# A mixture-of-experts backbone: the first expert in the order of the others, its slot weights in parts, and the last two experts added on chip

## The chip, the cores and the metric

The kernel runs on one core of a Trainium2 chip. The time is that of the device for one execution, in microseconds (us); less is better. The engines are TensorE (PE, matmuls), VectorE (DVE), ScalarE (ACT), GpSimd (POOL), and the queue engine SP, which issues most of the loads.

## What is computed

Two layers of a backbone over 256 context tokens and 512 latent tokens of width 1024. Each layer is a token mixer and a mixture of experts, each added to the residual. The mixture, cut to what matters here:

```python
g_top = argmax(h @ rg_w + rg_b)              # 1 of 4 groups, weight g_w
top_vals, top_idx = lax.top_k(e_in, 2)       # 2 of its 8 experts
top_w = softmax(top_vals) * g_w
...
def run_block(tok, e):                       # rows tok of h, expert e of 32
    xb = h_pad[tok]
    return (silu(xb @ w_gate[e]) * (xb @ w_up[e])) @ w_down[e]
...
y = segment_sum(y_buf * buf_w[:, None], buf_tok)
```

Each expert has a gate and an up matrix of 1024x512 and a down matrix of 512x1024 in f32, 6 MB together. Layer 0 has 768 tokens, layer 1 only needs the 512 latent ones. All 32 experts are computed in both.

## The kernel before

**Experts.** Every expert gets a table of 96 slots (`CAP`). `slots` makes, for all experts at once, which token stands in which slot (`si`); `values` makes what weight it has (`sv`, and `v4` for tokens that find no slot): DVE splits the weights into three f16 parts (`rwt`), PE places them by selection matrices (`ptab`, L1117), DVE adds the parts (`tw`, `sv`). `fetch` (POOL, an indirect DMA) reads an expert's rows from HBM into `xg`, `turn` transposes them on PE, `turned` copies them to `xh` (DVE) and `xl` (ACT). `gate_up` is the gate or the up product (`pgate`, `pup`); `act_gate`, `act_mult` and `act_split` make the activation, `at`; `down_mm` is the down product (`pdn`), `down_out` scales it by the slot weight on ACT, `scatter` gates it on POOL and adds it to the residual rows `xs` in HBM by an indirect DMA.

**Weights.** The weights come in halves of 1 MB into 7 buffers (`raw`, `NR`). The order of the loads is written out, and `pump` issues the next one on SP when a buffer is given back and no more than `depth` are under way. A half becomes two f16 matrices: `hi_` on ACT (L1337), then `lo_` on DVE (L1342), which frees the buffer. The second half of a down matrix is used in f32 by PE (`native`). In this document lo(up 1a) is the DVE conversion of the first half of expert 1's up matrix, gate(31) the gate product of expert 31.

**Order.** Nothing is scheduled by a tool: each engine executes its instructions in the order of the code. For expert e the loop computes act_mult(e), gate(e+1), the conversions for e+1 and e+2, pdn(e), the transposed rows of e+2, and up(e+1). Expert 0 stands ahead of the loop, in an order of its own: slot weights, transposes of expert 1, pdn(0), gate(1), up(1). The last two experts:

- Experts 0 to 30 are added to `xs` by scatters; then `load_latent` loads the latent rows from `xs` (SP) into `xl`.
- Expert 31 is added on chip (`last_down`, `add_last`): selections `pes` (`make_sel`, four on POOL at expert 28) are transposed on PE (`pst`, L1434), its product is placed by matmuls (`pcm`, L1458), and DVE adds them to the loaded rows (L1461).
- Between up(31) and pdn(31) stands `overflow_blocks`: each engine loads the number of overflow blocks and branches (L1357) over a loop for tokens that found no slot. There are none for this input.

Of the kernel before, what the change touches and what calls it, by code (L numbers as in the profile page):

```python
# [8 lines left out]
F32 = mybir.dt.float32  # L9
# [9 lines left out]
D = 1024  # L19
# [5 lines left out]
NE = 32  # L25
# [16 lines left out]
def kernel(ctx: ExitStack, tc: tile.TileContext, a: dict, out: bass.AP):  # L42
# [16 lines left out]
    def W(shape, dt, name="wt"):  # L59
        return pw.tile(shape, dt, name=name, tag="W")  # L60
# [970 lines left out]
    class Route:  # L1031
# [89 lines left out]
        def values(self):  # L1121

            nt, tmp, oh, v4 = self.nt, self.tmp, self.oh, self.v4
            g0, o1, o2, tv = tmp[:, :, 56:60], tmp[:, :, 120:152], tmp[:, :, 152:184], tmp[:, :, 184:216]
            gs, w1, w2, ex = (tmp[:, :, 220 + i] for i in range(4))

            def bc(x, n=32):
                return x.unsqueeze(2).to_broadcast([128, nt, n])

            V.tensor_tensor(g0, self.L[:, :, 32:36], bc(tmp[:, :, 40], 4), op=ALU.subtract)  # L1130
            V.tensor_tensor(ex, tmp[:, :, 49], tmp[:, :, 48], op=ALU.subtract)
            A.activation(g0, g0, AF.Exp)
            A.activation(ex, ex, AF.Exp)
            V.tensor_tensor(v4[:, :, :, 0], oh, bc(tokv[:, 0:nt]), op=ALU.mult)
            V.tensor_reduce(gs, g0, axis=AX.X, op=ALU.add)
            V.tensor_scalar(w1, ex, 1.0, None, op0=ALU.add)
            V.reciprocal(gs, gs)
            V.reciprocal(w1, w1)
            V.tensor_tensor(w1, w1, gs, op=ALU.mult)
            V.tensor_tensor(w2, w1, ex, op=ALU.mult)  # L1140
            rs = []
            for k, (o, w) in enumerate(((o1, w1), (o2, w2))):
                V.scalar_tensor_tensor(tv, o, VS, bc(w), op0=ALU.mult, op1=ALU.mult)
                rs.append(W([128, nt, 3, 32], F16, "rwt"))
                for q in range(3):
                    V.tensor_copy(rs[k][:, :, q], tv)
                    if q < 2:
                        V.tensor_tensor(tv, tv, rs[k][:, :, q], op=ALU.subtract)
            for q in range(3):
                V.tensor_tensor(v4[:, :, :, q + 1], rs[0][:, :, q], rs[1][:, :, q], op=ALU.add)  # L1150
            pt = self.table(rs, 96)
            t = W([128, 96], F32, "tw")[0:CAP]
            V.tensor_copy(t, pt)
            V.tensor_tensor(t[:, 0:32], t[:, 0:32], t[:, 32:64], op=ALU.add)
            V.tensor_tensor(t[:, 0:32], t[:, 0:32], t[:, 64:96], op=ALU.add)
            V.tensor_scalar(self.sv[0:CAP, 0], t[:, 0:32], IWS / VS, None, op0=ALU.mult)

        def overflow(self):

# [60 lines left out]
    def turn(xg):  # L1220

        out = []
        for r in range(2):
            pt = pp.tile([128, KC, CAP], F16, name="pgx", tag="P")
            for c in range(KC):
                o = r * D + c * 128
                T.transpose(pt[:, c, :], xg[0:CAP, o:o + 128], ident16[0:CAP, 0:CAP])
            out.append(pt)
        return out

    def turned(pts):
        xh = W([128, KC, CAP], F16, "xh")
        xl = W([128, KC, CAP], F16, "xl")
        V.tensor_copy(xh, pts[0])  # L1234
        A.copy(xl, pts[1])  # L1235
        return xh, xl
# [29 lines left out]
    def act_mult(pu, sg):  # L1266

        V.scalar_tensor_tensor(sg[:, 0:2], pu[:, 0:2], IWS, sg[:, 0:2], op0=ALU.mult, op1=ALU.mult)
        V.tensor_tensor(sg[:, 2:4], pu[:, 2:4], sg[:, 2:4], op=ALU.mult)

    def act_split(sg):
        at = W([128, 2, 2, CAP], F16, "at")
        A.copy(at[:, 0], sg[:, 0:2])  # L1273
        V.tensor_tensor(at[:, 1], sg[:, 0:2], at[:, 0], op=ALU.subtract)
        return at

    def down_mm(w, raw, at, sg, n):

        hi, lo = w
        sl = slice(n * 512, (n + 1) * 512)  # L1280
        pt = P([128, 512], "pdn")
        for f in range(2):
            mm3(pt[0:CAP, :], at[:, 0, f, :], at[:, 1, f, :], hi[:, f, sl], lo[:, f, sl], f == 0, False)
        for f in range(2, 4):
            T.matmul(pt[0:CAP, :], lhsT=sg[:, f, :], rhs=raw[:, f - 2, sl], start=False, stop=(f == 3))  # L1285
        return pt

    def down_out(pt, wcol, yt, n):
        A.activation(yt[0:CAP, n * 512:(n + 1) * 512], pt[0:CAP, :], AF.Copy, scale=wcol)  # L1289
# [55 lines left out]
    def moe(l, h2, rt, pe0, nt, post_load=None):  # L1345
# [3 lines left out]
        def overflow_blocks():  # L1349
# [7 lines left out]
            with tc.If(nov > 0):  # L1357
                with tc.For_i(0, nov) as _i:
# [17 lines left out]
                    V.tensor_tensor(pm, posm, eqb, op=ALU.mult)  # L1376
                    V.tensor_reduce(pb[:, :, 0], pm, axis=AX.X, op=ALU.add)
                    V.tensor_scalar(pb[:, :, 0], pb[:, :, 0], bc[:, 3:4], None, op0=ALU.subtract)
                    vb = W([128, nt, 4], F16, "vb2")
                    for q in range(4):  # L1380
                        V.tensor_tensor(pm, v4[:, :, :, q], eqb, op=ALU.mult)
                        V.tensor_reduce(vf, pm, axis=AX.X, op=ALU.add)
# [36 lines left out]
                            mm3(pt[0:CAP, :], at[:, 0, f, :], at[:, 1, f, :], hi[:, f, sl], lo[:, f, sl], f == 0, f == 3)  # L1419
                        down_out(pt, sv[0:CAP, 1:2], yg[:, 0, :], n)  # L1420
                    scatter(l, yg, si[0:CAP, :1], gs, V)
                load_latent(nc.gpsimd)

        xl = []

        def load_latent(eng=nc.sync):
            for i in range(4):
                eng.dma_start(out=xl[i // 2][:, i % 2, :], in_=xs[l][i * 128:(i + 1) * 128, :])
# [58 lines left out]
        def rows_of(e):  # L1487
            yg = yes[e % 2]
            return yg, gate_rows(yg, rt.sv[0:CAP, 1, e:e + 1], g2r, nv)
# [16 lines left out]
        gate_up(convs.pop((l, 0, 1)), xe, put)  # L1506
        lo_()
        hi_(1, 1, 0)
        act_mult(put, sg)
        at = act_split(sg)  # L1510
        lo_()
        rt.values()
        hi_(1, 1, 1)
        yg, gs = rows_of(0)
        w, raw = convs.pop((l, 0, 2)), natives.pop((l, 0))
        xt_ = turn(xg[:, 1])
        for n in range(2):
            pt = down_mm(w, raw, at, sg, n)
            if n == 0:
                xe = turned(xt_)  # L1520
            down_out(pt, weight(0), yg[:, 0, :], n)
        lo_()
        scatter(l, yg, slot(0), gs, Q)
        pgt = P([128, 4, CAP], "pgate")
        gate_up(convs.pop((l, 1, 0)), xe, pgt)
        hi_(2, 0, 0)
        sg = act_gate(pgt)
        lo_()
        hi_(2, 0, 1)
        xt_ = turn(xg[:, 0])  # L1530
        xn = turned(xt_)
        lo_()
        hi_(1, 2, 0)
        native(1)
        lo_()
        put = P([128, 4, CAP], "pup")
        gate_up(convs.pop((l, 1, 1)), xe, put)
        hi_(2, 1, 0)
        lo_()
        hi_(2, 1, 1)  # L1540
        for e in (3, 4):
            fetch(l, xg[:, e % 2], slot(e))
        xe = xn
        pes = None
        for e in range(1, NE):

            nx, nx2 = e + 1 < NE, e + 2 < NE
            act_mult(put, sg)
            at = act_split(sg)
            if lows:  # L1550
                lo_()
            sgd = sg
            w, raw = convs.pop((l, e, 2)), natives.pop((l, e))
            yg, gs = rows_of(e)
            if e == NE - 2:
                st["depth"] = NR - 2
            if e == NE - 4:
                pes = W([128, nt, CAP], F16, "pe")
                make_sel(pes, posm[:, :, NE - 1:NE], range(4))
            if not nx:  # L1560
                break
            pgt = P([128, 4, CAP], "pgate")
            gate_up(convs.pop((l, e + 1, 0)), xe, pgt)
            if nx2:
                for hf in range(2):
                    hi_(e + 2, 0, hf)
                    lo_()
            sg = act_gate(pgt)
            hi_(e + 1, 2, 0)
            native(e + 1)  # L1570
            lo_()
            pt = down_mm(w, raw, at, sgd, 0)
            down_out(pt, weight(e), yg[:, 0, :], 0)
            if nx2:
                hi_(e + 2, 1, 0)
            pt = down_mm(w, raw, at, sgd, 1)
            down_out(pt, weight(e), yg[:, 0, :], 1)
            scatter(l, yg, slot(e), gs, Q)
            if nx2:
                xn = turned(turn(xg[:, e % 2]))  # L1580
                lo_()
                hi_(e + 2, 1, 1)
                if e + 4 < NE:
                    fetch(l, xg[:, e % 2], slot(e + 4))
            else:
                xl += [G([128, 2, D], F32, "xl") for _ in range(2)]
                load_latent()
                selT = sel_transposed(pes)
                if post_load:
                    post_load()  # L1590
            put = P([128, 4, CAP], "pup")
            gate_up(convs.pop((l, e + 1, 1)), xe, put)
            xe = xn
            if e == 8:
                rt.overflow()
        overflow_blocks()
        if l == 0:
            st["depth"] = 4
            conv_w("win", 1, 4, 0)
# [1 line left out]
        yh = last_down(w, raw, at, sgd, yg, NE - 1, gs)  # L1601
        if l == 0:
            scatter_rows(l, yg, slot(NE - 1))
        add_last(selT, yh)
        return xl

    iot1 = pc.tile([128, CAP], F16, name="iot1")
# [190 lines left out]
```

## Time and profile before

| | |
|---|---|
| median of 3 runs | 1833.77 us (1828.28 to 1836.45) |
| the profiled execution | 1832.03 us |
| its span | 1830.3 us |
| busy: PE, PEld, DVE, ACT, POOL | 88%, 64%, 74%, 56%, 56% |
| mean DMA rate over the span | 296 GB/s |
| overall granted clock of TensorE | 0.944 |

The span is from the first to the last instruction. A window lists the engines in the order of the table, with their instructions in brackets; PEclk is the granted clock of TensorE as a share of 2.4 GHz (0.50 is 1.2 GHz). The busy shares are means over stages with different limits: the mixture of layer 0 lies at about 372 to 982 us, that of layer 1 at 1239 to 1820.

### The profile page before, as it was taken

What the parts mean: (1) busy time and instruction counts of PE and PEld (TensorE: products, weight loads), DVE (VectorE), ACT (ScalarE), POOL (GpSimd) and SP (SyncE); (2) the same over time, 40 slices, a digit from 0 to 9 for tenths busy, and PEclk for the clock granted to TensorE, in tenths of its full rate; (3) what the DMA queues carried; (4) which work ended last, traced back from release to release, by engine and by line L of the source; (5) the groups of instructions that cost most, each with busy time, mean ns of one, the idle gap of its engine ahead of it and who ended that gap; (6) DMA issues with size and microseconds to landing.
All of it is one profiled execution on the core that took longest, in us unless ns stands there. A gap on an engine that the chain in (4) does not pass through costs nothing. (4 is left out here: it accounts for less than half of the span.)

```text
span 1830.3 us, 43421 instructions
## 1 busy us (share of the span) xinstructions
PE 1610.0 (88%) x19059; PEld 1178.2 (64%) x19059; DVE 1346.8 (74%) x1453; ACT 1020.0 (56%) x1040; POOL 1030.3 (56%) x530
## 2 busy tenths in 40 slices
PE   6999999868888999888788999977987988899896
PEld 3577775556676777676664667546766676777663
DVE  5665566778768998777778777786876876777664
ACT  4433342446666676565654444345766676766763
POOL 1222224556998899988895233252555455665553
PEclk9999999988999999999998999988999999999998
DMA  9635455569998999999994354747999999999993
GB/s 386 240 135 187 162 209 200 172 206 365 362 369 318 372 394 387 369 351 358 364 353 174 113 198 167 299 154 234 409 386 371 361 384 365 370 387 369 371 359 122
DMA packets 127293, 542.33 MB, mean 296 GB/s; under 512 B 21594, under 2 KB 22666, under 8 KB 91000
## 3 DMA queue, kind: packets, MB, share of 16 engines
q1 hardware_dynamic: 105384, 507.87, 72.9%
q0 software_dynamic: 18000, 20.56, 4.7%
q10 hardware_dynamic: 3712, 11.04, 1.6%
q8 instruction: 153, 2.51, 0.5%
q14 instruction: 44, 0.36, 0.1%
HBM read 538.72 MB, written 45.69 MB: 319 GB/s over the span
## 5 line engine op out<-in xcount | busy, mean ns | idle before, releaser
L1342 DVE SCALAR_TENSOR_TENSOR wlo<-raw,whi 128x2048 f16<-128x2048 f32 x248 | 599.1, 2447 | 187.6 <-ACT whi L1337 187.3
L1337 ACT ACTIVATE whi<-raw 128x2048 f16<-128x2048 f32 x248 | 472.6, 1910 | 292.6 <-DMA raw<-in_exp_w_up_dram 245.0
L420 PEld LDWEIGHTS <-wlo 128*128 128x128 f16 x4512 | 457.3, 101 | 156.1 <-issue 124.8
L418 PEld LDWEIGHTS <-whi 128*128 128x128 f16 x4512 | 458.2, 102 | 45.5 <-issue 16.3
L419 PEld LDWEIGHTS <-whi 128*128 128x128 f16 x4512 | 457.6, 101 | 41.7 <-issue 12.6
L419 PE MATMUL pgate<-xl,whi 128*128 128x96 f16 x2048 | 305.1, 219 | 114.1 <-ACT xl L1235 113.7
L418 PE MATMUL pgate<-xh,whi 128*128 128x96 f16 x2048 | 309.0, 219 | 5.8 <-DVE xh L1234 5.7
L420 PE MATMUL pgate<-xh,wlo 128*128 128x96 f16 x2048 | 305.1, 219 | 0.0
L1305 POOL TENSOR_TENSOR ye<-ye,modrow 96x512 f32<-96x512 f32 x62 | 161.9, 2612 | 239.0 <-ACT ye L1289 239.0
L418 PE MATMUL pup<-xh,whi 128*128 128x96 f16 x2048 | 266.3, 206 | 0.0
L420 PE MATMUL pup<-xh,wlo 128*128 128x96 f16 x2048 | 266.1, 206 | 0.0
L419 PE MATMUL pup<-xl,whi 128*128 128x96 f16 x2048 | 266.0, 206 | 0.0
L1285 PE MATMUL pdn<-raw,sg 128*96 128x512 f32 x512 | 246.0, 604 | 0.0
L1309 POOL DMA_INDIRECT xs<-ye,si x63 | 183.3, 2910 | 22.5 <-POOL ye L1305 17.5
L1342 DVE SCALAR_TENSOR_TENSOR wd<-raw,wd 128x2048 f16<-128x2048 f32 x64 | 165.9, 2592 | 15.6 <-ACT wd L1337 15.4
L1305 POOL TENSOR_TENSOR ye<-ye 96x512 f32<-96x512 f32 x62 | 137.1, 2222 | 56.0 <-ACT ye L1289 54.0
L1296 POOL TENSOR_SCALAR ye<-modrow,sv 96x1024 f32<-96x1024 f32 x32 | 145.2, 4538 | 1.3
L1285 PEld LDWEIGHTS pdn<-raw,sg 128*96 128x96 f32 x512 | 85.6, 167 | 90.6 <-issue 71.9
L1337 ACT ACTIVATE wd<-raw 128x2048 f16<-128x2048 f32 x64 | 122.2, 1909 | 22.0 <-DMA raw<-in_exp_w_down_dram 22.0
L405 DVE SCALAR_TENSOR_TENSOR wlo<-raw,whi 128x2048 f16<-128x2048 f32 (+1 forms) x36 | 85.3, 2373 | 40.3 <-ACT whi L404 40.3
L418 PE MATMUL pdn<-wd,at 128*96 128x512 f16 x256 | 100.1, 391 | 16.4 <-ACT at L1273 8.6
L1215 POOL DMA_INDIRECT xg<-hs,si x62 | 91.6, 1477 | 32.5 <-issue 20.3
(310 smaller groups left out, 3103.3 us busy)
## 6 DMA issues: line engine op xcount, KB each, us to landing
raw<-in_exp_w_gate_dram SPq DMA_DIRECT2D x128, 1024.0 KB
raw<-in_exp_w_up_dram SPq DMA_DIRECT2D x128, 1024.0 KB
raw<-in_exp_w_down_dram SPq DMA_DIRECT2D x128, 1024.0 KB
raw<-in_ada_w_dram SPq DMA_DIRECT2D x32, 1024.0 KB
raw<-in_w_in_dram SPq DMA_DIRECT2D x20, 1024.0 KB
raw<-in_ada_dram SPq DMA_DIRECT2D x16, 1024.0 KB
raw<-in_w_out_dram SPq DMA_DIRECT2D x8, 1024.0 KB
xs<-xr ACTq DMA_DIRECT2D x10, 512.0 KB
```

The lines of the kernel that those rows point to most:

```text
L405: V.scalar_tensor_tensor(lo, t, WS, hi, op0=ALU.mult, op1=ALU.subtract)
L418: T.matmul(o, lhsT=lh, rhs=rh, start=first, stop=False)
L419: T.matmul(o, lhsT=lh, rhs=rl, start=False, stop=False)
L420: T.matmul(o, lhsT=ll, rhs=rh, start=False, stop=last)
L1215: Q.indirect_dma_start(out=xg, out_offset=None, in_=hs[l], in_offset=bass.IndirectOffsetOnAxis(ap=si, axis=0), bounds_check=(6 - 2 * l) * ...
L1285: T.matmul(pt[0:CAP, :], lhsT=sg[:, f, :], rhs=raw[:, f - 2, sl], start=False, stop=(f == 3))
L1296: Q.tensor_scalar(gn, g2r[0:CAP, 1, :], ctx, None, op0=ALU.mult)
L1305: eng.tensor_tensor(yn, yn, gs[n], op=ALU.mult)
L1309: Q.indirect_dma_start(out=xs[l], out_offset=bass.IndirectOffsetOnAxis(ap=si, axis=0), in_=yg[0:si.shape[0], 0, :], in_offset=None, bounds ...
L1337: A.activation(hi[:, sl, :], t, AF.Copy, scale=WS)
L1342: V.scalar_tensor_tensor(lo, t, WS, hi, op0=ALU.mult, op1=ALU.subtract)
```

## The change

1. Expert 0 goes through the same loop as the others. Ahead of it the rows of expert 1 are transposed first, and `values` becomes a generator with three parts: the weights and their split; `ptab`, `tw`, `sv`; and `v4`. The first runs at the loop's entry, the second and third behind the first and second conversion after gate(1).
2. `overflow_blocks` stands at the start of expert 29's turn. The scratch for its values is a part of another tile.
3. Experts 30 and 31 are both added on chip. The latent rows are loaded ahead of gate(31), behind the scatter of expert 29. The selections of both (8) are made by DVE there, and transposed there by PE. Expert 30 is scattered as well, after `last_down`. Its `add_last` stands between up(31) and pdn(31), where the branch stood.
4. `depth` falls to `NR - 2` two experts earlier.

```diff
@@ values
+            yield
             pt = self.table(rs, 96)
...
             V.tensor_scalar(self.sv[0:CAP, 0], t[:, 0:32], IWS / VS, None, op0=ALU.mult)
+            yield
+            V.tensor_tensor(v4[:, :, :, 0], oh, bc(tokv[:, 0:nt]), op=ALU.mult)
+            for q in range(3):
+                V.tensor_tensor(v4[:, :, :, q + 1], rs[0][:, :, q], rs[1][:, :, q], op=ALU.add)
+            yield
@@ overflow_blocks
                     scatter(l, yg, si[0:CAP, :1], gs, V)
-                load_latent(nc.gpsimd)
@@ moe
         hi_(1, 1, 0)
-        act_mult(put, sg)
-        at = act_split(sg)
+        xe = turned(turn(xg[:, 1]))
         lo_()
-        rt.values()
         hi_(1, 1, 1)
...
-        for e in range(1, NE):
+        vals = rt.values()
+        for e in range(NE):
...
-            if e == NE - 2:
+            if e == NE - 4:
                 st["depth"] = NR - 2
-            if e == NE - 4:
-                pes = W([128, nt, CAP], F16, "pe")
-                make_sel(pes, posm[:, :, NE - 1:NE], range(4))
+            if e == NE - 3:
+                overflow_blocks()
             if not nx:
                 break
+            if e == 0:
+                next(vals)
+            if e == NE - 2:
+                xl += [G([128, 2, D], F32, "xl") for _ in range(2)]
+                load_latent()
+                sels = []
+                for k in (NE - 2, NE - 1):
+                    pe = W([128, nt, CAP], F16, "pe")
+                    make_sel(pe, posm[:, :, k:k + 1], range(4), V)
+                    sels.append(sel_transposed(pe))
+                if post_load:
+                    post_load()
             pgt = P([128, 4, CAP], "pgate")
             gate_up(convs.pop((l, e + 1, 0)), xe, pgt)
             if nx2:
                 for hf in range(2):
                     hi_(e + 2, 0, hf)
                     lo_()
+                    if e == 0:
+                        next(vals)
...
             else:
-                xl += [G([128, 2, D], F32, "xl") for _ in range(2)]
-                load_latent()
-                selT = sel_transposed(pes)
-                if post_load:
-                    post_load()
+                yh = last_down(w, raw, at, sgd, yg, e, gs)
+                scatter_rows(l, yg, slot(e))
...
-        overflow_blocks()
+        add_last(sels[0], yh)
...
-        add_last(selT, yh)
+        add_last(sels[1], yh)
```

**What it moves at the head.** The order on DVE in layer 0, before: two conversions (`wlo`, L1342: lo(gate 1b), lo(up 1a)) stand about the activation of expert 0 (`sg`, `at`); then the slot weights in one piece, to `tw` and `sv`, and the copy of expert 1's rows, `xh`.

```order
L1342 SCALAR_TENSOR_TENSOR wlo<-raw,whi 128x2048
L1268 SCALAR_TENSOR_TENSOR sg<-pup,sg 128x192
L1269 TENSOR_TENSOR sg<-pup,sg 128x192
L1274 TENSOR_TENSOR at<-sg,at 128x192
L1342 SCALAR_TENSOR_TENSOR wlo<-raw,whi 128x2048
L1130 TENSOR_TENSOR rtmp<-rtmp 128x6x4
...
L1150 TENSOR_TENSOR rv_2717<-rwt 128x192 x3
L1153 COPY tw<-ptab 96x96
...
L1234 COPY xh<-pgx 128x768
L1342 SCALAR_TENSOR_TENSOR wlo<-raw,whi 128x2048 x2
```

The same place on DVE after the change:

```order
L1345 SCALAR_TENSOR_TENSOR wlo<-raw,whi 128x2048
L1237 COPY xh<-pgx 128x768
L1345 SCALAR_TENSOR_TENSOR wlo<-raw,whi 128x2048
L1271 SCALAR_TENSOR_TENSOR sg<-pup,sg 128x192
...
L1345 SCALAR_TENSOR_TENSOR wlo<-raw,whi 128x2048
L1130 TENSOR_TENSOR rtmp<-rtmp 128x6x4
...
L1345 SCALAR_TENSOR_TENSOR wlo<-raw,whi 128x2048
L1151 COPY tw<-ptab 96x96
...
L1345 SCALAR_TENSOR_TENSOR wlo<-raw,whi 128x2048
L1156 TENSOR_TENSOR rv_2717<-roh,cf 128x192
L1158 TENSOR_TENSOR rv_2717<-rwt 128x192 x3
```

The copy of expert 1's rows moved from behind the slot weights to ahead of the activation of expert 0, and conversions stand between the weights' parts.

**What it moves in the tail.** The order on DVE in layer 1 after the change, from the copy of expert 31's rows (`xh`) to the last adds (`xl`); `pe` are the selections, `ye` and `yh` the gated product of an expert:

```order
L1237 COPY xh<-pgx 128x768
L1345 SCALAR_TENSOR_TENSOR wlo<-raw,whi 128x2048
L1271 SCALAR_TENSOR_TENSOR sg<-pup,sg 128x192
...
L1277 TENSOR_TENSOR at<-sg,at 128x192
L1345 SCALAR_TENSOR_TENSOR wlo<-raw,whi 128x2048
L1187 TENSOR_SCALAR pe<-iot_128,rp_15031 128x96 x8
L1345 SCALAR_TENSOR_TENSOR wd<-raw,wd 128x2048
L1448 SCALAR_TENSOR_TENSOR ye<-pdn,sv_15034,modrow 96x512 x2
...
L1463 TENSOR_TENSOR xl<-pcm,xl 128x512 x8
L1448 SCALAR_TENSOR_TENSOR ye<-pdn,sv_15034,modrow 96x512 x2
L1450 TENSOR_TENSOR yh<-ye,yh 96x512
L1463 TENSOR_TENSOR xl<-pcm,xl 128x512 x8
```

The eight selections, `ye` of expert 30 and eight adds are new there; the selections stand behind the activation of expert 30 and one conversion. On PE in layer 1 the eight transposes stand between up(30) and gate(31):

```order
L420 MATMUL pup<-xh,wlo 128x96
L1436 LDWEIGHTS pe
L1436 MATMUL pst<-ident_114,pe 96x128
...
L418 LDWEIGHTS whi
L418 MATMUL pgate<-xh,whi 128x96
```

Before, four of them stood between pdn(30) and up(31):

```order
L1285 MATMUL pdn<-raw,sg 96x512 x2
L1434 LDWEIGHTS pe
L1434 MATMUL pst<-ident_114,pe 96x128
...
L418 LDWEIGHTS whi
L418 MATMUL pup<-xh,whi 128x96
```

So gate(31) moved from a place right behind up(30) to one behind the selections' transposes.

## Rows read from the trace of the kernel before

**Rows 1.** Windows by stage; columns: us, each engine's busy us, PEclk, DMA share, GB/s

```profile
372.00:435.00 63.00, 45.01 (x694) 35.78 (x692) 52.41 (x74) 34.01 (x31) 29.75 (x16) 0.84 0.75 267
...
1290.00:1757.00 467.00, 412.46 (x6075) 323.67 (x6073) 341.13 (x259) 315.96 (x266) 260.95 (x108) 0.97 0.99 376
1757.00:1822.00 65.00, 51.89 (x604) 36.36 (x602) 35.44 (x37) 31.51 (x35) 29.47 (x16) 0.92 0.59 205
```

**Rows 2.** Waits of ACT, 435 to 960 us (us in total, times, longest).

```profile
ACT whi L1337 <- DMA raw<-in_exp_w_up_dram: 123.6, 44, 6.1
```

**Rows 3.** Waits of PE, head of layer 0 (376 to 430 us).

```profile
PE ptab L1117 <- DVE rwt L1146: 13.8, 2, 12.5
PE pdn L418 <- ACT at L1273: 4.1, 1, 4.1
```

**Rows 4.** Waits of PE, head of layer 1 (1240 to 1290 us).

```profile
PE ptab L1117 <- DVE rwt L1146: 9.3, 2, 8.1
```

**Rows 5.** Waits of PE, tail of layer 1 (1755 to 1822 us).

```profile
PE pdn L418 <- PEq L1357: 4.2, 1, 4.2
PE pgate L419 <- ACT xl L1235: 3.9, 1, 3.9
```

**Rows 6.** Timeline of DVE, head of layer 0 (start us, us, line, operation).

```profile
384.25 2.32 DVE L1130 TENSOR_TENSOR rtmp<-rtmp 128x24 f32<-128x24 f32 x1
...
389.83 2.48 DVE L1148 TENSOR_TENSOR rtmp<-rtmp,rwt 128x192 f32<-128x192 f32 x1
...
395.27 1.44 DVE L1150 TENSOR_TENSOR rv<-rwt 128x192 f16<-128x192 f16 x3
...
406.81 2.29 DVE L1342 SCALAR_TENSOR_TENSOR wlo<-raw,whi 128x2048 f16<-128x2048 f32 x1 [6.70 <-ACT whi L1337]
```

**Rows 7.** DMA issues between 379.2 and 381 us (count, us to landing).

```profile
xg<-hs,si POOLq DMA_INDIRECT x1, 8.1
```

**Rows 8.** Timeline of POOL, head of layer 0.

```profile
379.35 1.61 POOL L1215 DMA_INDIRECT xg<-hs,si  x1 [7.16 <-issue]
```

**Rows 9.** The line of the branch, PE's part (ns min/median/max).

```profile
L1357 PEldq COMPARE_BRANCH  x2: 3587/3988/4390, 961.1 to 1800.8; - x2
```

**Rows 10.** Waits of PE, tail of layer 0 (920 to 985 us).

```profile
PE pgate L419 <- ACT xl L1235: 3.7, 2, 2.4
```

**Rows 11.** Timeline of DVE, tail of layer 1.

```profile
1786.89 0.35 DVE L1268 SCALAR_TENSOR_TENSOR sg<-pup,sg 128x192 f32<-128x192 f32 x1
...
1788.27 2.29 DVE L1342 SCALAR_TENSOR_TENSOR wlo<-raw,whi 128x2048 f16<-128x2048 f32 x1
...
1815.43 4.86 DVE L1461 TENSOR_TENSOR xl<-pcm,xl 128x512 f32<-128x512 f32 x8
```

**Rows 12.** The line of the selections, those on DVE.

```profile
L1184 DVE TENSOR_SCALAR ph<-iot,rtmp x20: 237/242/247, 373.7 to 1241.4; 128x96 f16<-128x96 f16 x20
```

**Rows 13.** Timeline of DVE, tail of layer 0.

```profile
945.00 3.65 DVE L1342 SCALAR_TENSOR_TENSOR wlo<-raw,whi 128x2048 f16<-128x2048 f32 x1 [0.23 <-ACT whi L1337]
...
951.16 2.28 DVE L1342 SCALAR_TENSOR_TENSOR wlo<-raw,whi 128x2048 f16<-128x2048 f32 x1
...
964.89 8.01 DVE L405 SCALAR_TENSOR_TENSOR wlo<-raw,whi 128x2048 f16<-128x2048 f32 x2 [1.31 <-ACT whi L404]
```

**Rows 14.** Timeline of PE, first waiting matmul of gate(31) in layer 0.

```profile
946.27 0.20 PE L419 MATMUL pgate<-xl,whi 128*128 128x96 f16 x1 [1.26 <-ACT xl L1235]
```

**Rows 15.** Windows in the tail of layer 1, columns as in rows 1.

```profile
1767.80:1774.60 6.80, 5.16 (x66) 5.16 (x65) 5.95 (x6) 6.36 (x7) 5.53 (x2) 0.50 1.00 390
...
1805.40:1808.70 3.30, 3.25 (x7) 1.61 (x8) 0.00 (x0) 0.00 (x0) 0.00 (x0) 0.50 0.64 184
```

**Rows 16.** The chain that ended last (start us, us, what).

```profile
1810.25 0.22 PE pdn L418
...
1811.55 1.73 PE pdn L1285 x4
```

**Rows 17.** DMA queues, 1796 to 1806 us (packets, MB, share).

```profile
q8 instruction: 3, 0.05, 2.7%
```

More of the change, by code (lines that the diff above doesn't have):

```diff
@@ L1133, in values @@
             A.activation(ex, ex, AF.Exp)
-            V.tensor_tensor(v4[:, :, :, 0], oh, bc(tokv[:, 0:nt]), op=ALU.mult)
             V.tensor_reduce(gs, g0, axis=AX.X, op=ALU.add)
@@ L1148, in values @@
                         V.tensor_tensor(tv, tv, rs[k][:, :, q], op=ALU.subtract)
-            for q in range(3):
-                V.tensor_tensor(v4[:, :, :, q + 1], rs[0][:, :, q], rs[1][:, :, q], op=ALU.add)
+            yield
             pt = self.table(rs, 96)
@@ L1378, in overflow_blocks @@
                     V.tensor_scalar(pb[:, :, 0], pb[:, :, 0], bc[:, 3:4], None, op0=ALU.subtract)
-                    vb = W([128, nt, 4], F16, "vb2")
+                    vb = wt[:, 288:288 + 2 * nt].bitcast(F16).rearrange("p (t q) -> p t q", q=4)
                     for q in range(4):
@@ L1508, in moe @@
         hi_(1, 1, 0)
-        act_mult(put, sg)
-        at = act_split(sg)
+        xe = turned(turn(xg[:, 1]))
         lo_()
-        rt.values()
         hi_(1, 1, 1)
[L1514 to L1544, printed above, removed]
-        for e in range(1, NE):
+        vals = rt.values()
+        for e in range(NE):
             nx, nx2 = e + 1 < NE, e + 2 < NE
@@ L1571, in moe @@
             lo_()
-            pt = down_mm(w, raw, at, sgd, 0)
-            down_out(pt, weight(e), yg[:, 0, :], 0)
             if nx2:
+                pt = down_mm(w, raw, at, sgd, 0)
+                down_out(pt, weight(e), yg[:, 0, :], 0)
                 hi_(e + 2, 1, 0)
[L1576 to L1579, printed above, removed]
+                pt = down_mm(w, raw, at, sgd, 1)
+                down_out(pt, weight(e), yg[:, 0, :], 1)
+                scatter(l, yg, slot(e), gs, Q)
                 xn = turned(turn(xg[:, e % 2]))
@@ L1582, in moe @@
                 hi_(e + 2, 1, 1)
+                if e == 0:
+                    fetch(l, xg[:, 1], slot(3))
                 if e + 4 < NE:
```

## The prediction, made before the changed kernel ran

> **What bounds the kernel now.** I read the stages first, since the mean over the span mixes them. The windows by stage show the two MoE layers in three parts each [rows 1]: over the long middle (1290 to 1757 us in layer 1) the DMA share is 0.99, at 376 GB/s, while TensorE (PE) is busy for 412 of 467 us. The chip is waiting there for expert weights; in layer 0 the waits of ScalarE (ACT) say the same, 123.6 us in 44 waits for the landing of an up matrix [rows 2]. So a gain in the middle is worth nothing unless a weight load is issued earlier. At the head of a layer (372 to 435) the DMA share is 0.75 and at the tail (1757 to 1822) 0.59: there the engines' chain sets the pace, and both places are what the change edits. Next I read PE's waits in a head: 13.8 us in two waits for the slot weights (`ptab` on `rwt`), then 4.1 us for `at` [rows 3]; in layer 1 it is 9.3 us [rows 4]. Last, PE's waits in the tail: one of 4.2 us at the overflow branch [rows 5].
>
> **Head, layer 0.** VectorE (DVE) works on the slot weights from 384.25 to 396.7, and of the conversions behind them the second stands at 406.81 [rows 6]. A conversion frees a raw buffer, and so issues the next load. Now the transposes of expert 1's rows come first, then `xh`, lo(up 1a), act_mult(0), lo(up 1b), and the weights in three parts with conversions between. Expert 1's rows need 8.1 us to land [rows 7] from 379.35, where POOL issues their fetch [rows 8], so they are there at 387.5, and `xh` at about 389: DVE now idles some 6 us that it did not. Then lo(up 1a) ends at 391.3 (2.29 us a conversion [rows 6]), act_mult and `at` at 393.1, lo(up 1b) at 395.4. The first part of the weights is these 12.4 us less the four `rv` products (1.44 for three of them), so 10.5 at most; two of its instructions took 2.32 and 2.48 us [rows 6], which I read as GpSimd (POOL) at work beside them: in layer 1 PE waits only 9.3 us in all for the same work [rows 4]. POOL will be done by then, so I take half, 5.1. lo(gate 2a) then starts at 400.5 instead of 406.81, lo(gate 2b) and lo(down 1a) some 5 to 7 us earlier. Against that, up 2a's load, which waits for lo(up 1a), is issued at 391.3 instead of 384.3, and PE reaches pdn of expert 0 about 4 us later (it needs the slot weights, done at 401). The loads that follow are 3 to 5 us earlier, and as the middle is limited by the loads, that is kept: **-3.5 us**, bounds -8 (all that the conversions gain) and -1.
>
> **Head, layer 1.** The same order, but with less to be moved: PE's waits for the weights are 9.3 us instead of 13.8 [rows 3, 4]. The rows land about as long after their issue as in layer 0 [rows 7], which is later than DVE came to act_mult(0) here, so act_mult(0) slips by some 8 us, `ptab` by 11, and pdn of expert 1 by about 2.7 us, while the conversions behind come 3 us earlier. Loads that are earlier by 2 to 3 us and a PE that is later nearly cancel: **-1 us**, bounds -4 and +2.5.
>
> **The branch moved to expert 29.** On PE the compare-and-branch took 3.59 and 4.39 us [rows 9], and in the tail of layer 1 PE stood idle 4.2 us for it before pdn of expert 31 [rows 5]. Before gate(30) PE already waits 3.9 us (layer 1) for `xl` [rows 5], and 2.4 in layer 0 [rows 10]; the moved branch lies beside that wait, so it costs 0.3 and 1.1 us there. Without that cover it would be the full 4. On ACT, DVE and POOL the branch is about 1 us; on SP, in front of up 31b, d 31a and 31b, it waits for loads already landing, behind a full DMA queue. [...]
>
> **Selections on DVE, transposes before gate(31).** This is the large term. In layer 1, gate(31) starts right behind up(30), whose result DVE takes up at 1786.89 [rows 11]. In the new order its place on PE is behind eight transposes of selections that DVE makes after act_mult(30), `at` and lo(up 31b). DVE does that conversion from 1788.27 to 1790.56 [rows 11]; eight selections at 0.24 us, the ends of which overlap, add 1.3 to 1.9 [rows 12], the last transposes 0.3: gate(31) starts at about 1792.3, **+5.5**, less 0.4 for the four transposes that stood later. In layer 0 DVE is behind already: lo(up 31a) takes from 945.00 to 948.65, lo(up 31b) from 951.16 to 953.44 [rows 13], selections to 955; gate(31) at 955.6 instead of 946.27 [rows 14]: **+9.4**, less 0.4. After a gap like that PE's granted clock fell in this trace: 0.50 over 6.8 us after the 3.9-us wait before gate(30), and 0.50 over 3.3 us after the branch [rows 15]; at 1.2 instead of 2.4 GHz half of such a stretch is lost, so I add 2 in each layer (0 to 3.4).
>
> **Expert 30 added on chip.** Sixteen `pcm` matmuls stand between up(31) and pdn(31). A 512-column matmul of pdn took 0.217 us at the full clock (1810.25 to 1811.55 for six [rows 16]): 3.5 us. They fill the time in which `at`(31) is made, and in which the branch stood, 4.2 [rows 5]: net -0.7 in layer 1 and 0 in layer 0. pdn(31) then runs at the full clock, for PE is not idle ahead of it, and gets back half of the 3.3 us at 0.50 [rows 15]: **-1.6** in layer 1 and -0.4 in layer 0, where less of pdn lay in such a stretch. DVE's eight more adds of 0.61 us [rows 11] go beside PE. In layer 0 two conversions of w_in, which took 8.01 us [rows 13], now stand behind those adds and ahead of `ye` of expert 31: nothing if they run at 2.3 us each, 3 if not. The scatter of expert 30 and the earlier load of the latent rows lie behind nothing on the path.
>
> **Sum.** Tail of layer 1: 5.5 - 0.4 + 2 - 0.7 - 1.6 + 0.3 = +5 (bounds +3, clock at no cost, and +7). Tail of layer 0: 9.4 - 0.4 + 2 - 0.4 + 1.1 - 1.5 (POOL's selections at expert 28 are gone, and with them some of the 3.65 us of lo(up 31a), where 2.29 is the usual) = +10 (bounds +6 and +14, w_in included); what follows in layer 1's mixer waits for the latent rows, so nothing gives it back. Heads: -4.5. Together +10.5 (bounds -3 and +22.5). The profiled execution took 1832.0 us (span 1830.3 and 1.7 around it), 1.7 under the median of the runs, 1833.8: the forecast is 1844 by the median.
>
> **Rivals.** (1) The heads carry whole, faster: if PE and not the loads held the start of the layers, the waits of [rows 3, 4], 17.9 and 9.3 us, would all go: -27 and +15, 1822. It decides if the DMA queue is not full for some tens of us after a head. Against it: the share of 0.99 in the middle [rows 1], and the new wait for the fetched rows. 0.08. (2) No change: the heads keep their upper bound of -12, or the stall before gate(31) is smaller, since POOL and DVE run ahead in layer 0 once four selections have left POOL; +0 to +8, 1838. For it: DVE's two conversions in layer 0 stand 2.5 us apart [rows 13], so it is not full there. 0.32. (3) Slower than forecast: the taken branch fetches code, and at expert 29 the DMA engines are full (0.99) where at the end they were not. The trace shows three packets, 0.05 MB, of the instruction queue about the branch in layer 1 [rows 17]. If each fetch waits 4 us behind weights, PE starts gate(30) later in both layers: 1852. For it speaks only that the queue is full; against it that the branch was shorter (3.59) in layer 0, where w_in loads, than in layer 1 (4.39) [rows 9]. 0.08. [...] (4) The idle time at the end is not the branch's: then `pcm` lies inside it, and the 0.7 and the 2.0 us of pdn's clock are not won: 1847. Against it: the branch's 4.39 us and the 4.2 that PE waits are one time [rows 5, 9]. 0.04.
>
> **How the numbers follow.** The forecast, +6 to +16 about +10.5, has 0.48. A measurement of this kernel cannot tell less than about 0.5%, 9.2 us, from no change. Of the forecast's 0.48 I put 0.36 above that; with (3) and (4) slower is 0.48. Same is (2) and the rest of the forecast: 0.44. Faster 0.08. The range 1831 to 1856 takes the bounds of the sum but for its last microsecond, and leaves out (1) and the ends.
>
> **What would show it.** In the new profile: PE idle of 5 us before gate(31) in layer 1 and 9 in layer 0, put down to the selections; no wait at the branch before pdn(31); clock 1.0 in pdn(31); PE's 12.5-us wait for `rwt` split into one for the fetched rows and one for `rwt`. I am wrong if gate(31) starts within 2 us of up(30), or if the loads of the middle begin 8 us or more earlier against the layer's start.

## The result, and the profile after

The changed kernel takes 1858.88 us in the median (1855.4 to 1859.92), the kernel before, run beside it, 1834.87: a ratio of 1.0134 (95% interval 1.0106 to 1.0163), 24 us slower. The profiled execution took 1858.86 us with a span of 1857.0, 26.7 more than the span of before.

I cut both spans at PE's first matmul of gate(0) and its last of up(29), gate(30), gate(31), up(31) and pdn(31) in each layer, as the timeline of PE has them. Times between cuts, in us:

| | ahead | layer 0: to up(29) | gate(30) | gate(31) | up(31) | pdn(31) | mixer | layer 1: to up(29) | gate(30) | gate(31) | up(31) | pdn(31) | rest |
|---|---|---|---|---|---|---|---|---|---|---|---|---|---|
| before | 371.3 | 555.4 | 6.7 | 17.1 | 10.9 | 11.5 | 264.1 | 528.5 | 10.6 | 14.9 | 10.3 | 12.0 | 17.0 |
| after | 375.2 | 554.9 | 12.7 | 24.0 | 10.1 | 9.5 | 265.0 | 530.9 | 16.1 | 22.0 | 10.1 | 9.5 | 17.0 |

The two tails take 10.2 and 9.9 us more, the heads with their middles -0.5 and +2.4. The 3.9 us ahead of layer 0 lie in code that is the same, and the executions below have 369.7 to 375.8 there, with either head. PE's granted clock differs there: from 340 to 370 us it is 0.83 in the eight executions with 369.7 to 371.3, and 0.71 to 0.76 in the five with 372.5 to 375.8. Two windows of before (columns as in [rows 1]):

```profile
345.00:350.00 5.00, 5.00 (x18) 2.04 (x17) 2.97 (x3) 4.92 (x6) 0.55 (x1) 0.72 0.96 310
365.00:371.00 6.00, 5.86 (x95) 5.14 (x93) 5.86 (x9) 1.47 (x3) 5.14 (x5) 0.72 0.33 78
```

The same windows of after:

```profile
345.00:350.00 5.00, 5.00 (x15) 2.18 (x15) 2.41 (x3) 5.00 (x6) 0.55 (x1) 0.50 0.99 306
365.00:371.00 6.00, 4.00 (x40) 2.85 (x37) 5.66 (x19) 2.68 (x3) 4.80 (x5) 0.50 0.20 81
```

PE's waits in the tail of layer 1 after (the answer to [rows 5]; us in total, times, longest):

```profile
PE pgate L418 <- ACT whi L1340: 5.8, 1, 5.8
PE pst L1436 <- DVE pe L1187: 3.6, 1, 3.6
PE pgate L419 <- issue: 2.4, 1, 2.4
```

And those in the tail of layer 0 (to [rows 10]):

```profile
PE pgate L418 <- ACTq L1360: 6.0, 1, 6.0
PE pst L1436 <- DVE pe L1187: 5.3, 2, 4.5
```

The wait at the branch ahead of pdn(31) is gone. In its place stand 5.8 and 6.0 us ahead of gate(30), 2.4 us inside gate(30) for which the profile names nothing ("issue"; the experiments on the branch come back to it), and 3.6 and 5.3 us for the selections (`pst` on `pe`). The first wait of layer 1 is put down to ACT's `whi`, but it ends with the branch. The branch's own row (to [rows 9]) shows that on PE it takes longer here than at the end:

```profile
L1360 PEldq COMPARE_BRANCH  x2: 5932/5972/6012, 929.7 to 1781.8; - x2
```

Windows over gate(30) and pdn(31) of layer 1 (columns as in [rows 1]; to [rows 15]) show the clock that follows: 0.51 over gate(30) and 1.00 in pdn(31).

```profile
1788.00:1798.40 10.40, 7.91 (x97) 7.69 (x98) 7.06 (x5) 3.97 (x3) 3.94 (x2) 0.51 0.77 259
1834.00:1840.00 6.00, 6.00 (x21) 2.73 (x20) 3.30 (x6) 0.63 (x1) 1.15 (x1) 1.00 0.00 0
```

DVE in the tail of layer 1 (to [rows 11]): the conversion, then eight selections in 1.32 us.

```profile
1810.32 2.28 DVE L1345 SCALAR_TENSOR_TENSOR wlo<-raw,whi 128x2048 f16<-128x2048 f32 x1
1812.53 1.32 DVE L1187 TENSOR_SCALAR pe<-iot,rp 128x96 f16<-128x96 f16 x8
```

PE's waits in the head of layer 0 (to [rows 3]) are 14.6 us where they were 17.9; two thirds are now waits for fetched rows, the second of them for expert 3's, whose fetch POOL issues behind the scatter of expert 0:

```profile
PE pgx L1230 <- DMA xg<-hs,si: 9.8, 2, 6.3
PE ptab L1117 <- DVE rwt L1145: 4.2, 2, 2.6
PE pgate L419 <- ACT xl L1238: 0.6, 1, 0.6
```

POOL's timeline there, the scatter of expert 0 and the fetch of expert 3's rows:

```profile
416.68 3.39 POOL L1312 DMA_INDIRECT xs<-ye,si  x1 [0.28 <-POOL ye L1308]
420.37 2.45 POOL L1218 DMA_INDIRECT xg<-hs,si  x1 [0.30 <-issue]
```

### The profile page after: what moved, and what is told of

The parts are those of the page before. It is cut to its first block, busy times and chain, and to the rows that moved or that the text cites. A ratio compares the mean times of both kernels' runs of the same rounds, so it can differ in the third digit from the quotient of the medians.

```text
span 1857.0 us, 43540 instructions
## 1 busy us (share of the span) xinstructions
PE 1630.2 (88%) x19099; PEld 1198.7 (65%) x19099; DVE 1360.2 (73%) x1491; ACT 1021.6 (55%) x1042; POOL 1024.7 (55%) x520
## 5 line engine op out<-in xcount | busy, mean ns | idle before, releaser
L420 PEld LDWEIGHTS <-wlo 128*128 128x128 f16 x4512 | 464.3, 103 | 149.6 <-issue 118.2
L418 PEld LDWEIGHTS <-whi 128*128 128x128 f16 x4512 | 465.4, 103 | 57.6 <-issue 16.3
L419 PEld LDWEIGHTS <-whi 128*128 128x128 f16 x4512 | 464.7, 103 | 45.7 <-issue 16.0
L419 PE MATMUL pgate<-xl,whi 128*128 128x96 f16 x2048 | 321.2, 224 | 110.2 <-ACT xl L1238 107.5
L418 PE MATMUL pgate<-xh,whi 128*128 128x96 f16 x2048 | 324.8, 224 | 18.6 <-DVE xh L1237 6.7
L420 PE MATMUL pgate<-xh,wlo 128*128 128x96 f16 x2048 | 321.1, 224 | 0.0
L1288 PE MATMUL pdn<-raw,sg 128*96 128x512 f32 x512 | 241.6, 594 | 0.0
L1312 POOL DMA_INDIRECT xs<-ye,si x63 | 178.5, 2833 | 17.4 <-POOL ye L1308 16.6
L1299 POOL TENSOR_SCALAR ye<-modrow,sv 96x1024 f32<-96x1024 f32 x32 | 147.3, 4602 | 1.3
L1218 POOL DMA_INDIRECT xg<-hs,si x62 | 95.7, 1543 | 35.1 <-issue 23.0
L419 PE MATMUL pjl<-hTl,whi 128*128 128x512 f16 x256 | 97.7, 382 | 3.1 <-DVE hTl L448 3.1
```

The costliest lines, as they stand in the source:

```text
L418: T.matmul(o, lhsT=lh, rhs=rh, start=first, stop=False)
L419: T.matmul(o, lhsT=lh, rhs=rl, start=False, stop=False)
L420: T.matmul(o, lhsT=ll, rhs=rh, start=False, stop=last)
L1218: Q.indirect_dma_start(out=xg, out_offset=None, in_=hs[l], in_offset=bass.IndirectOffsetOnAxis(ap=si, axis=0), bounds_check=(6 - 2 * l) * ...
L1299: Q.tensor_scalar(gn, g2r[0:CAP, 1, :], ctx, None, op0=ALU.mult)
L1312: Q.indirect_dma_start(out=xs[l], out_offset=bass.IndirectOffsetOnAxis(ap=si, axis=0), in_=yg[0:si.shape[0], 0, :], in_offset=None, bounds ...
```

## The experiments

Each edit is against the kernel that the sentence names. Ratios are to the kernel before, run beside it. The cuts are those of the table above.

**The two halves of the change.** e1 is the kernel before with the new head, e2 with the new tail; their diffs are the head's and the tail's lines of the diff above.

> The kernel before with the new head alone (parts of the slot weights, expert 0 in the loop). Theory A, the head gains by earlier loads: at equal megabytes landed, the weights of layer 0's middle come 3 to 4 us earlier against the layer's start, those of layer 1 about 2, and the time is 1828 to 1835 (ratio 0.996 to 1.000). Rival B, the new head slows the middle (its new wait for fetched rows, a later fetch of expert 3): the middle lasts 3 to 4 us longer in each layer, 1838 to 1842.

> The kernel before with the new tail alone (branch at expert 29, last two experts added on chip, selections on DVE). Theory A: tails of 11 and 10 us more than before, 1855 to 1858, as slow as the whole change. Rival B, part of the loss is the head's: 1848 to 1850.

e1: 1834.67 us, ratio 0.9995 (0.9976 to 1.0015). e2: 1858.87 us, 1.0133 (1.0108 to 1.0158). So the whole loss is the tail's (in e2's profile 13.8 and 9.3 us of it, where 11 and 10 were expected), and the head alone changes nothing that can be measured. Summing the landed packets of SP's queue, the first 115 MB of the program were there 145.2 us after gate(0) of layer 0 began, as the mean of the eight kernels here with the new head (143.9 to 147.6), and 147.3 in the five with the old (146.3 to 148.6): a gain of 2 us in loads. In layer 1 there is none: counted from its gate(0), the first 380 MB were there after 204.3 and 203.5 us. To up(29) of layer 0 one of the 2 us is left in these means (555.3 and 556.3), and in layer 1 it is 530.9 and 529.6, while single executions differ by 7. The time of e1 is in theory A's range, but the loads gain less than the 3 to 4 and 2 us that it counted on, and the little that they gain does not show in the time. PE's waits in the head of e1 show what came in the place of the weights' wait:

```profile
PE pgx L1230 <- DMA xg<-hs,si: 11.3, 2, 6.7
PE ptab L1117 <- DVE rwt L1145: 3.8, 2, 2.5
```

And in the tail of e2, the three waits for selections in layer 0; the other line, put down to DVE's `sg`, is the stand at the branch, which runs there from 926.26 to 932.25 us:

```profile
PE pst L1433 <- DVE pe L1184: 10.4, 3, 5.0
...
PE pgate L418 <- DVE sg L1269: 6.2, 1, 6.2
```

**The transposes' place.** e4, against the changed kernel:

```diff
-                sels = []
+                pes = []
                 for k in (NE - 2, NE - 1):
...
-                    sels.append(sel_transposed(pe))
+                    pes.append(W([128, nt, CAP], F16, "pe"))
...
                 scatter_rows(l, yg, slot(e))
+                sels = [sel_transposed(pe) for pe in pes]
```

> The changed kernel with the eight transposes of the selections behind pdn(30) instead of ahead of gate(31); the selections stay where they are on DVE. Theory A, the transposes' place is the stall: gate(31) starts right behind up(30) in layer 1 and within 2 us in layer 0, 12 to 15 us less than the changed kernel. Rival B, DVE's chain of act, conversion and selections is the limit wherever the transposes stand (it moves to pdn(30)): 4 us less at most.

e4: 1844.68 us, ratio 1.0062 (1.0038 to 1.0085), 14 us less than the changed kernel. gate(31) ends 14.9 and 15.0 us after gate(30) instead of 24.0 and 22.0 (17.1 and 14.9 in the kernel before). Theory A holds. Part comes back in layer 0, whose mixer takes 270.1 instead of 265.0: there PE waits for `yh` of expert 31, late on DVE behind the adds of expert 30 and the w_in conversions:

```profile
PE pcm L1460 <- ACT yh L1449: 5.1, 1, 5.1
```

**The branch.** e3 is the changed kernel without `overflow_blocks()`; e7 has in its place, at expert 29,

```diff
-                overflow_blocks()
+                _, vals2 = nc.values_load_multi_w_load_instructions(
+                    rt.novi[0:1, 0:1], engines=mybir.ALL_ENGINES, min_val=0, max_val=16)
...
+                with tc.If(vals2[0] > 0):
+                    V.memset(bc[:, 1:2], -1.0)
```

> The changed kernel without the overflow branch (it leaves out the overflow blocks, of which there are none). Theory A, the code behind the taken branch is fetched while DMA is full, and PE stands for it ahead of gate(30): PE's idle there falls from 5.8 and 6.0 us to 2.4 to 3.9, the 2.4 us inside gate(30) of layer 1 go, no half clock in gate(30) of layer 0; 8 to 11 us less than the changed kernel. Rival B, PE waits there for the rows of ACT in any case: at most 3 us less.

> The changed kernel with a branch at expert 29 over one small DVE instruction in place of the overflow blocks, which it leaves out. Theory A, the 6 us on PE are the fetch of code from beyond the overflow blocks: the compare-and-branch of PE takes under 0.5 us, PE waits ahead of gate(30) for the rows as without a branch, and the time is that of the kernel without the branch, 1850 to 1854. Rival B, the 6 us are the branch's own, or its load of the number, at a full DMA queue: they stay, 1857 to 1861.

e3: 1852.61 us, 1.010 (1.0071 to 1.013). e7: 1854.81 us, 1.0094 (1.0074 to 1.0114). In layer 1 gate(30) ends 10.2 and 9.4 us after up(29) instead of 16.1, so the branch cost 6 us there. The whole time of e3 is 6.3 us less than that of the changed kernel, between what theory A (8 to 11) and rival B (at most 3) had, because layer 0 gave nothing back, as shown below; e7 is 1 us above theory A's range and well under rival B's. Over a small body PE's compare-and-branch is a fifth of a microsecond:

```profile
L1532 PEldq COMPARE_BRANCH  x2: 207/222/236, 927.4 to 1785.8; - x2
```

So the branch is cheap and the 6 us depend on what it jumps over. The packets of the instruction queue (q8) point to what is waited for. The DMA queues of the changed kernel while PE stands at the branch in layer 1, 1781.8 to 1787.8 us (packets, MB, share):

```profile
q1 hardware_dynamic: 541, 2.44, 98.9%
q8 instruction: 1, 0.02, 1.1%
```

That packet of 16 KB lands at 1786.19 us, and the branch ends at 1787.73. All sixteen readings over the overflow blocks (eight kernels, two layers each) end like this, 1.41 to 1.54 us after such a packet has landed; in e7 none lands while PE is at the branch. The "issue" gaps inside gate(30) of layer 1 (2.4, 2.5, 1.2 and 0.7 us in after, e2, e4 and e6) end 1.34 to 1.56 us after the next one, so I read them as a second fetch. The branch's rows on ACT, DVE, POOL and SP stay at 0.05 to 0.07 us; by the kernel's code, PE has the most instructions in the block. That PE waits there for a fetch of the code behind the block is my reading of these packets and of e7. The shortest row over the overflow blocks, 3.50 us, is 15 times the longer of the two over the small body, 0.24 us.

In layer 0 the loss did not go with the branch: gate(30) is 3.6 and 5.5 us earlier, but gate(31) 6.4 and 9.3 us later after it. PE's waits in the tail of layer 0 of e3 show where:

```profile
PE pst L1436 <- DVE pe L1187: 11.1, 3, 5.8
PE pgate L419 <- ACT xl L1238: 7.6, 2, 4.4
```

The wait for `up` 31a is part of it: its load lands hardly earlier without the branch (ACT takes it up 17.6 us after up(29) in e3, 18.4 in the changed kernel), and DVE's activation and selections stand behind that conversion. Then the selections took 6.93 us on DVE, one of them 4.05, about the scatter of expert 29 on POOL. The timeline of DVE of e3:

```profile
952.77 6.93 DVE L1187 TENSOR_SCALAR pe<-iot,rp 128x96 f16<-128x96 f16 x8
```

The line of the selections in e3, all on DVE (ns min/median/max):

```profile
L1187 DVE TENSOR_SCALAR pe<-iot,rp x26: 119/242/4053, 362.2 to 1809.9; 128x96 f16<-128x96 f16 x26
```

The timeline of POOL in e3, that scatter and the row work behind it:

```profile
950.68 3.65 POOL L1312 DMA_INDIRECT xs<-ye,si  x1 [0.28 <-POOL ye L1308]
953.85 3.39 POOL L1299 TENSOR_SCALAR ye<-modrow,sv 96x1024 f32<-96x1024 f32 x1
```

e11 is e3 without that scatter, and its selections stand in the timeline of DVE behind the expectation:

> The changed kernel without the overflow branch and, in layer 0, without the scatter of expert 29 (it leaves out the overflow blocks and adds nothing of expert 29 to layer 0). Theory A, one selection of DVE took 4 us in layer 0 because POOL was issuing this scatter beside it: the eight selections take 1.3 to 3 us instead of 6.9, and gate(31) of layer 0 ends 4 us earlier after gate(30) than with the scatter. Rival B, POOL's row work stretches them in any case: at most 1.5 us earlier.

```profile
955.41 2.81 DVE L1187 TENSOR_SCALAR pe<-iot,rp 128x96 f16<-128x96 f16 x8
```

The selections took 2.81 us, so with the scatter in its place they are 4 us longer. What holds them is not the issue alone. In e3 three selections that ran beside it took 0.24 us each; the fourth began at 953.23, 1.1 us before the issue ended, and ended at 957.28, 0.04 us after POOL's next instruction, the row work (953.85 + 3.39 = 957.24). In e2 and e7 it is the same to 0.04 us. Without the scatter that row work starts ahead of the selections, so e11 moves it too, and which of the two it is stays open. The other half of the expectation missed as it was put: gate(31) ends only 1.1 us earlier after gate(30), but PE did not wait in gate(30) in that execution. Counted from up(29), gate(31) ends after 33.8 us in e11 and 39.5 in e3; 1.1 us of the difference is an earlier load of up 31a. 1850.79 us, 1.0086.

**The branch in the kernel before.** e5 leaves it out; e6 moves it to expert 29. With it `depth` falls at expert 28, and POOL's four selections move from expert 28 to 29, behind the branch, which the expectation does not say.

> The kernel before without its overflow branch (it leaves out the overflow blocks, of which there are none). Theory A, at the end of the experts the branch costs what PE stands beyond the making of at(31), 2.4 and 3.0 us, and the half clock of pdn(31) behind it, 0.4 and 1.6: 5 to 8 us faster, 1826 to 1829. Rival B, ACT and DVE are as late there without it: at most 2 us faster.

> The kernel before with the branch alone moved to expert 29 (and the fall of depth with it). Theory A, the branch takes 6 us on PE there, of which the wait for the rows hides 2.4 to 4: it loses 3 to 5 us in each layer there and wins 2.8 and 4.6 at the end, 1831 to 1838. Rival B, as the prediction had it, it is hidden there: 1826 to 1829.

e5: 1829.62 us, 0.9969 (0.9954 to 0.9984): 6.4 us less. e6: 1834.95 us, 0.9989 (0.9966 to 1.0012). Theory A holds twice, with e5 half a us above the range of its time. In e6 gate(30) ends 12.5 and 12.9 us after up(29) where e5 has 6.9 and 9.8, and pdn(31) 8.6 and 7.1 after up(31), where before has 11.5 and 12.0. Moving the branch to expert 29 trades one place for the other. PE's waits in the tail of layer 0 of e6 have the 6.0 us, and nothing at the end but `at`:

```profile
PE pgate L418 <- PEq L1357: 6.0, 1, 6.0
...
PE pdn L420 <- DVE at L1274: 1.3, 1, 1.3
PE pdn L418 <- ACT at L1273: 0.9, 1, 0.9
```

**Expert 30 on chip by itself.** e8 is e4 without the branch, and with the w_in conversions ahead of the adds of expert 30:

```diff
-        add_last(sels[0], yh)
         if l == 0:
...
             conv_w("win", 1, 4, 1)
+        add_last(sels[0], yh)
```

> The changed kernel with the transposes of the selections behind pdn(30), the two w_in conversions of layer 0 ahead of the adds of expert 30, and no branch (it leaves out the overflow blocks). Theory A, with the three losses gone, the head's 3 us and the time that the sixteen matmuls of expert 30 take from waiting are left: 1826 to 1833, within 5 us of the kernel before without its branch. Rival B, adding expert 30 on chip costs by itself (its sixteen matmuls and eight adds): 1836 or more.

1837.48 us, 1.0003 (0.9992 to 1.0015), which is 8 us more than e5, the kernel before without its branch: rival B's range. In layer 1 pdn(31) ends 9.5 us after up(31) instead of 7.1, since sixteen matmuls stand where only `at`(31) was waited for. In layer 0 it is 17.1 instead of 8.2; my own edit is part of that, for PE waits for DVE's adds to give up PSUM, so only the 2.4 us of layer 1 are clean of it:

```profile
PE pdn L418 <- DVE xl L1463: 4.7, 1, 4.7
```

With the adds first (e4) that wait is gone and `yh` of expert 31 is late instead. Either order has a wait of about 5 us in layer 0.

**The branch in the middle.** e9 is the kernel before, e10 the same with the new head, with the branch at expert 16:

```diff
-                    fetch(l, xg[:, 0], si[:, :1])
+                    xo = G([128, 2 * D], F16, "xo")
...
-            if e == NE - 2:
+            if e in (15, NE - 2):
                 st["depth"] = NR - 2
...
+            if e == 16:
+                overflow_blocks()
+                st["depth"] = NR
...
-        overflow_blocks()
```

> The kernel before with the branch at expert 16, in the middle of a layer (with a buffer of its own for the overflow's rows, and depth at NR - 2 during expert 15). Theory A, PE's 6 us there are paid out of its waits, since the weights' landing sets the pace: as fast as without a branch, 1827 to 1831. Rival B, the branch also stops SP, which waits there for the landing of its loads; the DMA queue runs empty and the middle lasts 3 to 10 us longer in each layer: 1836 to 1850.

> The new head, the tail of before and the branch at expert 16. Theory A, the head's 3 us in layer 0 and the branch's 6 add up: 1824 to 1830, ratio 0.993 to 0.998. Rival B, as for the branch at expert 16 alone, or the head's gain is given back in the middle: 1831 or more.

e9: 1829.23 us, 0.9976 (0.9959 to 0.9993). e10: 1829.12 us, 0.9962 (0.9947 to 0.9977), the lowest medians here of kernels with all their work, 0.2 and 0.4% under the kernel before and 30 us under the changed one. e9 is as fast against the kernel before as e5, which has no branch (0.9969), and its pdn(31) ends 8.8 and 7.1 us after up(31), as in e6. The branch of e9 is as long as at expert 29:

```profile
L1357 PEldq COMPARE_BRANCH  x2: 6002/6075/6148, 683.5 to 1539.4; - x2
```

And PE stands for it, as its waits in the middle of layer 1 (1290 to 1757 us) show, first in before, then in e9:

```profile
PE pgate L419 <- ACT xl L1235: 54.4, 23, 4.8
...
PE pgate L419 <- ACT xl L1235: 44.1, 19, 4.5
PE pgate L418 <- PEq L1357: 5.8, 1, 5.8
```

But up(29) of layer 1 ends 527.7 us after gate(0) began, no later than in before (528.5) and e5 (531.6). PE is ahead of the weights there, and the 5.8 us come out of its waits for the next rows, which are 10 us shorter. In layer 0 it is less clean. The DMA share dips some 15 us behind the branch, in e9 and in e10, where SP waits 11.3 us for a buffer that DVE's conversion of a down matrix gives back. As a mean the middle hardly shows it (363 GB/s, 365 in before), but up(29) of layer 0 ends 558.1 us after gate(0) where before and e5 have 555.4 and 555.3: some 3 us of rival B, in one execution (windows of e9):

```profile
705.00:720.00 15.00, 12.08 (x171) 9.04 (x168) 12.94 (x9) 14.47 (x13) 11.86 (x5) 1.00 0.72 269
...
435.00:960.00 525.00, 450.32 (x6476) 353.30 (x6474) 416.09 (x275) 336.01 (x283) 466.66 (x173) 0.95 0.97 363
1290.00:1757.00 467.00, 417.01 (x6082) 329.31 (x6080) 340.34 (x259) 315.37 (x266) 254.88 (x107) 0.95 0.99 375
```

Whether the head adds to that is not settled: e9 and e10 differ by less than their intervals. No execution here enters the overflow blocks, so these times are those of the path that skips them.

## Why the prediction was wrong

The direction and the large term were right, the size was not: +24 where +10.5 was forecast and +22.5 was the upper bound. Of the 13.5 us that are missing, the branch in the tail of layer 1 is about 5 and the heads 4.5; the rest is no more than single executions differ by, and its place is not shown. The tail of layer 0 came out as forecast (10.2 where 10 was the sum) by luck: the branch was dearer and the selections cheaper than their terms. Of the signs, the wait at the branch before pdn(31) is gone and its clock is 1.0, as said; the waits put down to the selections are 3.6 and 5.3 us, not 5 and 9.

- **Selections ahead of gate(31).** Forecast 7.1 us in layer 1 with the clock; measured 22.0 - 14.9 = 7.1, and 7.0 from e4 to after. In layer 0 forecast 11, or 9.5 with the 1.5 us for POOL's selections; measured 24.0 - 14.9 = 9.1 against e4, and 24.0 - 17.1 = 6.9 against before. This step stood.
- **The branch at expert 29: the step that failed.** "The moved branch lies beside that wait, so it costs 0.3 and 1.1 us there." It cost 16.1 - 10.2 = 5.9 us in layer 1 (against e3) and 12.7 - 9.1 = 3.6 in layer 0, where removing it gave nothing back, since the load of up 31a and the selections became the limit. I took 3.59 and 4.39 us from [rows 9], where the DMA share over the branch itself was 0.58 and 0.34, for the price where it is 1; over the branch at experts 29 and 16 the share is 0.93 to 1.03, and PE's branch took 5.93 to 7.09 us in all twelve readings (after, e2, e4, e6, e9 and e10, two layers each). And the wait of 3.9 us did not cover it: against before, gate(30) of layer 1 is 5.5 us longer, 1.9 by the stand itself (5.8 for 3.9), 2.4 by the gap inside gate(30), and the 1.2 that are left go with a longer stretch at half clock. Rival (3) had the mechanism, a fetch of code that waits some 4 us, with +8 us and a chance of 0.08; e7 and the packets agree with it. The packet on which PE's branch ends starts 1.01 to 1.05 us after the branch at the end of a layer (four readings) and 3.39 to 4.60 after it at experts 29 and 16 (twelve). That it starts late because the DMA engines are full fits all sixteen but was not tried by itself.
- **The end of the experts.** Forecast -2.3 in layer 1 and -0.4 in layer 0; measured 9.5 - 12.0 = -2.5, and -2.0. Rival (4) is out: without the branch (e5) the wait before pdn(31) is 1.6 and 0.9 us, for `at`, instead of 3.6 and 4.2.
- **The heads.** Forecast -4.5; e1 shows 0 (interval -4.4 to +2.8). In layer 0 the loads were earlier, by 2 us where 3 to 5 were worked out, and in layer 1 not at all; PE's pdn(0) was 4 us later after gate(0), as worked out (405.2 - 375.2 against 397.1 - 371.3). Where the 2 us went is not shown. I priced the wait for expert 1's rows but not the second one for expert 3's.
- **What I did not see.** In layer 0 a selection on DVE can fall on POOL's scatter and the row work behind it and take 4 us (e2, e3, e7). The adds of expert 30 delay the w_in conversions or pdn(31): the "nothing, or 3" was about 1 in the changed kernel, whose mixer takes 265.0 instead of 264.1, and about 5 in e4 and e8.

## What to carry to other kernels

Here a branch over a long body held the engine with the most code in it for 3.5 to 7.1 us at each of the three places where it was tried; put such a branch where that engine is ahead of what sets the pace (here the DMA-bound middle), and not where it is merely seen to wait in the old order. Before work is moved ahead of a critical product, list what stands in front of its inputs on their engine: eight selections of 1.3 us in all cost 7 because an activation and a conversion came first. A price that was read in one place need not be the price in another: the same branch took 3.59 and 4.39 us at the end of a layer and 5.9 to 7.1 where the DMA share was near 1.

## What the runs showed of the hardware

- PE's compare-and-branch takes 0.21 and 0.24 us over one DVE instruction, 3.50 to 4.39 us over the overflow blocks at the end of a layer, 5.93 to 7.09 at experts 29 and 16, with a DMA share of 0.93 to 1.03. In all sixteen readings over the overflow blocks it ends 1.41 to 1.54 us after a 16-KB packet of the instruction queue has landed.
- A DVE selection of 128x96 f16 takes 0.24 us, and 4.05 us where it ends with POOL's row work behind an indirect DMA (e2, e3, e7).
- POOL's issue of that DMA took 3.65 us where a conversion on DVE had begun 0.11 us ahead of it (e2, e3, e7), and 1.60 where the issue began first (after, 954.14 us; e4, 949.65 us). Which of the two engines begins first goes with the length in these five readings; what makes the issue longer was not shown.
- The 512-column f16 matmuls of pdn(31) in layer 1 of before begin 0.427 us apart where the granted clock was 0.50 (six from 1805.45 to 1808.01 us) and 0.215 us apart where it was 1.00 (six from 1810.09 to 1811.38 us). That is 1.20 and 2.38 columns a ns, and all that the traces show of the 1.2 and 2.4 GHz named ahead of the result; the clock itself they give as a share.
- The same code ahead of layer 0 differs by 6 us between executions (369.7 to 375.8), and the slower executions have PE at the lower granted clock there (0.71 to 0.76 from 340 to 370 us, against 0.83).
